# Output projection of a hybrid decoder layer by Strassen's seven products, weight sums formed on GpSimd beforehand

## The chip, the cores and the metric

One core of a Trainium2 chip runs the kernel. The metric is the device time of one execution in microseconds (us). Engines are named as in the profile: PE is TensorE (matmuls; PEld its weight loads), DVE VectorE, ACT ScalarE, POOL GpSimd, SP SyncE, which here issues most transfers. Each engine works through its own list of instructions in order; semaphores make it wait for the others.

## The reference, cut to what matters

```
h = rmsnorm(x, norm_pre_g)                      # x: 512 x 2048, float32
qa, ka, va, za, qb, ckv, zb, iq, ik, iw = split(h @ w_in)
o_a = diff_attention(qa, ka, va, ...)           # 8 heads: (softmax1 - lam*softmax2) @ v, rmsnorm of each head
o_b = dsa_attention(qb, ckv, iq, ik, iw, ...)   # 8 heads: 128 keys of 512 for each query, picked by an indexer
y = concat(o_a * silu(za), o_b * silu(zb)) @ w_out     # (512 x 2048) @ (2048 x 2048)
out = x + rmsnorm(y, norm_post_g)
```

Every weight is used in full float32 accuracy: a product A @ B is made as Ah@Bh + Ah@Bl + Al@Bh, where Ah is A rounded to the fast matmul format and Al the rest.

## The kernel before, in words

Everything is kept transposed, 128 features by 512 positions in a tile. **Weights** come in *units* of 128 x 1024 numbers (512 KB). `units` lists them in order of use; `load_to` issues the load from SP's queue (L98) into one of two tiles wf, `split_to` rounds it on ACT into wh (L124) and subtracts on DVE into wl (L125), `use` hands out the next pair and keeps three units split ahead. A weight tile and an activation tile give three matmuls.

**Stages.** First ckv, the index queries and keys, the 16 gates (tiles go0 to go15, SiLU applied), then 16 rounds that find the 128 best keys on DVE (L377, L378); before them POOL masks the three score tiles sc1 to sc3 (L371). Then 8 heads of group A (`head_a`): projections, two softmaxes, values into the PSUM bank av, and the norm of the head: PE sums squares (L518), DVE scales them (L193), POOL raises to the power -1/2 (`rstd`, L194, tile ro), PE spreads the four columns over the bank (`spread`, L200), and DVE multiplies into go[h]. Then 8 heads of group B (`head_b`). POOL has hardly anything else: the relative-bias strips go through DRAM tables that POOL writes early (L336).

**Output projection.** go0 to go15 are split into pairs hh, hl. Four column blocks n of 512; in each, 8 units of two 128-row weight tiles meet four position tiles i: 24 matmuls of 128x512 per unit (L606 to L608), 768 in all (some cut in halves of 256 columns at the very end). ACT squares a finished bank for the norm (L612), DVE multiplies it with the gain (L614). The last block goes position tile by position tile (L648 to L650), so that the norm, the scaled sum with x (L665) and the store (L666) of one tile run beside the matmuls of the next.

**Order of the work.** The program is written as straight code; a scheduler with tile dependencies and priorities places each instruction in its engine's list, so an engine that is free early gets later code early. In the loops over heads the code is written in the order projection, attention, norm.

Of the kernel before, what the change touches and what calls it, by code (L numbers as in the profile page):

```python
# [8 lines left out]
OP = mybir.AluOpType  # L9
# [16 lines left out]
def hybrid_layer(tc, xT, xn, wck, wT, wik, wva, wuv, wo, gpre, gpost, sub, kvg, ikg, lq1, lk1, lq2, lk2, relb, oneh, out):  # L26
    nc = tc.nc
    from contextlib import ExitStack
    with ExitStack() as st:
# [50 lines left out]
        for n in range(4):  # L80
            for kp in range(8):
                unit(wo[n, kp], (2, 512))
        stage, ready, flags = {}, {}, {"begin": None}
# [5 lines left out]

        def load_to(n):  # L90
            while pos["load"] < min(n, len(units)):
                i = pos["load"]
                ap, shp = units[i]
                c = shp[0] * shp[1]
                nm, bf = ("wf", 2) if flags["begin"] is not None else ("qk", 4)
                t = S.tile([128, 1024], F32, name=nm, bufs=bf)
                with tc.high_priority(lead()):
                    nc.sync.dma_start(t[:, :c], ap)  # L98
                stage[i] = t
                pos["load"] += 1  # L100

        last = [("qk", 4)] * 4 + [("v", 3)] * 3 + [("ck0", 1), ("ck1", 1)] + [("wh", 3), ("wl", 3)] * 3 + [("pt0a", 1)]

        def split_to(n):
            while pos["split"] < min(n, len(units)):
                i = pos["split"]
                load_to(i + 1)
                c = units[i][1][0] * units[i][1][1]
                t = stage.pop(i)
                names = [("wh", 3), ("wl", 3)]  # L110
                if i >= len(units) - 8:
                    names = [last.pop(0), last.pop(0)]
                w = []
                for nm, bf in names:
                    if nm == "pt0a":
                        w.append([S.tile([128, 512], F32R, name=x, bufs=1) for x in ("pt0a", "pt0b")])
                    else:
                        a = S.tile([128, 1024], F32R, name=nm, bufs=bf)
                        w.append([a[:, :512], a[:, 512:]] if units[i][1][1] == 512 else [a[:, :c]])
                m = c // len(w[0])  # L120
                with tc.high_priority(lead()):
                    for q in range(len(w[0])):
                        src = t[:, q * m:(q + 1) * m]
                        nc.scalar.copy(w[0][q], src)  # L124
                        nc.vector.tensor_tensor(w[1][q], src, w[0][q].bitcast(F32), op=OP.subtract)  # L125
                ready[i] = w
                pos["split"] += 1

        def use(ahead=3):
            i = pos["use"]  # L130
            pos["use"] += 1
            if ahead:
                load_to(i + ahead + 1)
                split_to(i + ahead)
            nk, n = units[i][1]
            w = ready.pop(i)
            per = nk // len(w[0])
            return [[w[a][k // per][:, (k % per) * n:(k % per + 1) * n] for k in range(nk)] for a in range(2)]
# [370 lines left out]
        def head_a(h, q, k, kl):  # L509
# [3 lines left out]
            sq = tmp("sq", 1)  # L513
# [38 lines left out]

        for h in range(8):
            next(sel, None)
            if h % 2 == 0:
                project_va(h // 2)
            t = scaled(proj_T(), 0.125)
            q = pair("qk", 4)
# [9 lines left out]
            next(sel, None)  # L568
            head_a(h, q, k, kl)
        for _ in sel:  # L570
            pass

        oh_, ol_ = [], []

        def split_o(m):
            a = S.tile([128, 512], F32R, name=f"hh{m}")
            b = S.tile([128, 512], F32R, name=f"hl{m}")
            split((a, b), go[m])
            oh_.append(a)
            ol_.append(b)  # L580

        for h in range(8):
            if h % 2 == 0:
                project_vb(h // 2)
            q = [project_qk(1.0 / 16), project_qk(1.0 / 16)]
            if h == 7:
                for m in range(15):
                    split_o(m)
            head_b(h, q)
        split_o(15)  # L590


        ssy = S.tile([128, 4, 4], F32, name="ssy")
        ys = {}
        for n in range(4):
            gB = S.tile([128, 512], F32, name="strip", bufs=2)
            nc.gpsimd.dma_start(gB, bcast(gpost[n], 512))
            if n % 2 == 0:
                banks = [proj_bank(), proj_bank(), proj_bank(), lg_bank()]
            else:  # L600
                banks = [lg_bank(), tr_bank(), tr_bank(), av_bank()]
            def part(kp, i, wh, wl):
                ts = slice(i * 128, (i + 1) * 128)
                for k in range(2):
                    kk = 2 * kp + k
                    nc.tensor.matmul(banks[i], oh_[kk][:, ts], wh[k], start=(kk == 0), stop=False)  # L606
                    nc.tensor.matmul(banks[i], oh_[kk][:, ts], wl[k], start=False, stop=False)  # L607
                    nc.tensor.matmul(banks[i], ol_[kk][:, ts], wh[k], start=False, stop=(kk == 15))  # L608

            def done(i):  # L610
                junk = S.tile([128, 512], F32, name="a3")
                nc.scalar.activation(junk, banks[i], AF.Square, accum_out=ssy[:, i, n:n + 1])  # L612
                y = S.tile([128, 512], F32, name=f"go{i * 4 + n}")
                nc.vector.tensor_tensor(y, banks[i], gB, op=OP.mult)  # L614
                ys[i, n] = y

            if n < 3:
                for kp in range(8):
# [3 lines left out]
                for i in range(4):  # L622
                    done(i)
                continue
            ws = []
            for i in range(4):
                xs = []
                for q in range(4):
                    xr = S.tile([128, 512], F32, name="e" if q < 2 else "tq", bufs=2)
                    nc.sync.dma_start(xr, xn[i * 128:(i + 1) * 128, q * 512:(q + 1) * 512])  # L630
                    xs.append(xr)
                y = S.tile([128, 512], F32, name=f"go{i * 4 + n}")
                ys[i, n] = y
                base = S.tile([128, 1], F32, name="base", bufs=2)
                nc.vector.tensor_reduce(base, ssy[:, i, :3], axis=mybir.AxisListType.X, op=OP.add)
                nc.vector.tensor_scalar(base, base, 1.0 / D, EPS, op0=OP.mult, op1=OP.add)
                ry = S.tile([128, 1], F32, name="ry", bufs=2)
                cuts = (0, 512) if i < 3 else (0, 256, 512)
                for a, b in zip(cuts, cuts[1:]):
                    o = (banks[i] if a == 0 else proj_bank())[:, a:b]  # L640
                    for kp in range(8):
                        if i == 0:
                            ws.append(use())
                        wh, wl = ws[kp]
                        for k in range(2):
                            kk = 2 * kp + k
                            ts = slice(i * 128, (i + 1) * 128)
                            nc.tensor.matmul(o, oh_[kk][:, ts], wh[k][:, a:b], start=(kk == 0), stop=False)  # L648
                            nc.tensor.matmul(o, oh_[kk][:, ts], wl[k][:, a:b], start=False, stop=False)
                            nc.tensor.matmul(o, ol_[kk][:, ts], wh[k][:, a:b], start=False,  # L650
                                             stop=(kk == 15))
                    junk = S.tile([128, 512], F32, name="a3")
                    sl = ssy[:, i, 3:4]
                    nc.scalar.activation(junk[:, :b - a], o, AF.Square, accum_out=sl)
                    nc.vector.scalar_tensor_tensor(ry if b == 512 else base, sl, 1.0 / D, base,
                                                   op0=OP.mult, op1=OP.add)
                    nc.vector.tensor_tensor(y[:, a:b], o, gB[:, a:b], op=OP.mult)
                nc.gpsimd.tensor_tensor(ry, ry, mhalf[:, 0:1], op=OP.pow)
                for q in range(4):
                    if i == 3 and q == 1:  # L660
                        t = S.tile([128, 512], F32, name="sq", bufs=1)
                        nc.scalar.activation(t, ys[i, q], AF.Copy, scale=ry)
                        nc.gpsimd.tensor_tensor(ys[i, q], t, xs[q], op=OP.add)
                    else:
                        nc.vector.scalar_tensor_tensor(ys[i, q], ys[i, q], ry, xs[q], op0=OP.mult, op1=OP.add)  # L665
                    nc.sync.dma_start(out[i * 128:(i + 1) * 128, q * 512:(q + 1) * 512], ys[i, q])  # L666
# [67 lines left out]
```

## Time and profile before

| | us |
|---|---|
| runs (3) | median 1059.06, 1058.71 to 1059.2 |
| profiled execution | 1059.01, its span 1057.1 |
| PE / DVE / ACT / POOL busy | 1043.6 / 567.5 / 421.2 / 35.0 |
| granted clock of PE, mean share of full speed | 0.996 |
| DMA | 116.09 MB, mean 110 GB/s |

Busy time of PE overlaps: a matmul of 512 columns is listed with 0.39 us, but the next one starts 0.23 us after it. "Chain" is the work that ended last, followed back from the end: a share of PE there is time that only PE could shorten. A name like pj or go is a tile; L is a line of the kernel before.

### The profile page before, as it was taken

How to read it: one execution, taken by the hardware profiler on the slowest of the kernel's cores; microseconds unless marked ns; L12 is line 12 of the kernel's file. 1: busy time of each engine (PE TensorE's matmuls, PEld its weight loads, DVE VectorE, ACT ScalarE, POOL GpSimd, SP SyncE). 2: the span in 40 equal slices, each digit the busy share in tenths (PEclk: the TensorE clock that was granted, in tenths of full speed). 3: DMA queues.
4: the chain of work that ended last, by engine and by line, in shares of the span. 5: the costliest groups of instructions: out<-in, count | busy, mean ns of one | idle time of the engine just before them, and what ended most of it. 6: DMA issues, size and time to landing. Idle time of an engine off the chain costs nothing.

```text
span 1057.1 us, 13923 instructions
## 1 busy us (share of the span) xinstructions
PE 1043.6 (99%) x5425; PEld 898.9 (85%) x5425; DVE 567.5 (54%) x1144; ACT 421.2 (40%) x789; POOL 35.0 (3%) x57
## 2 busy tenths in 40 slices
PE   8999999999999999999999999999999999999996
PEld 6798898888889899899899888888888888888886
DVE  5355554469953565465465466554645484323443
ACT  6543433332222564464365365332323353322320
POOL 2002100000000000000000000000000000000001
PEclk9999999999999999999999999999999999999999
DMA  8625723232333222222222232222222232333445
GB/s 295 237 97 152 250 100 100 100 100 80 100 100 100 85 85 91 80 90 80 91 90 70 90 99 91 71 97 73 90 80 90 80 100 90 101 100 110 139 130 189
DMA packets 37265, 116.09 MB, mean 110 GB/s; under 512 B 4592, under 2 KB 4720, under 8 KB 37200
## 3 DMA queue, kind: packets, MB, share of 16 engines
q1 hardware_dynamic: 35280, 108.68, 31.3%
q0 software_dynamic: 1920, 6.53, 2.2%
q8 instruction: 42, 0.69, 0.3%
q14 instruction: 23, 0.19, 0.1%
HBM read 110.96 MB, written 9.48 MB: 114 GB/s over the span
## 4 chain that ended last, share of the span: by engine, by line
PE 97%; DMA 1%; SPq 0%; DVE 0%; issue 0%; ACT 0%; DVEq 0%; POOL 0%; ACTq 0%; POOLq 0%
PE pj L161 19%; PE pj L160 19%; PE pj L159 19%; PE pj L451 3%; PE pj L450 3%; PE pj L449 3%; PE lg L534 3%; PE av L432 3%; PE pj L606 2%; PE pj L608 2%; PE pj L607 2%; PE lg L256 2%; PE lg L258 2%; PE tr L421 2%; PE lg L608 1%; PE lg L606 1%
## 5 line engine op out<-in xcount | busy, mean ns | idle before, releaser
L161 PE MATMUL pj<-hh,wl 128*128 128x512 f32 (+2 forms) x912 | 351.8, 386 | 0.0
L160 PE MATMUL pj<-hl,wh 128*128 128x512 f32 (+2 forms) x912 | 350.6, 384 | 0.0
L159 PE MATMUL pj<-hh,wh 128*128 128x512 f32 (+2 forms) x912 | 350.5, 384 | 0.0
L124 ACT CAST wh<-wf 128x1024 fp32r<-128x1024 f32 (+2 forms) x181 | 164.7, 923 | 394.9 <-PE pj L160 186.4
L125 DVE TENSOR_TENSOR wl<-wf,wh 128x1024 fp32r<-128x1024 f32 (+2 forms) x181 | 191.2, 1067 | 206.0 <-ACT wh L124 205.8
L161 PEld LDWEIGHTS pj<-hh,wl 128*128 128x128 f32 (+1 forms) x912 | 170.7, 187 | 30.8 <-issue 0.9
L160 PEld LDWEIGHTS pj<-hl,wh 128*128 128x128 f32 (+1 forms) x912 | 170.7, 187 | 30.1
L159 PEld LDWEIGHTS pj<-hh,wh 128*128 128x128 f32 (+1 forms) x912 | 170.8, 187 | 29.4
L451 PE MATMUL pj<-wh,hl 128*128 128x256 f32 x256 | 72.9, 285 | 0.0
L449 PE MATMUL pj<-wh,hh 128*128 128x256 f32 x256 | 72.9, 285 | 0.0
L450 PE MATMUL pj<-wl,hh 128*128 128x256 f32 x256 | 72.7, 284 | 0.0
L262 DVE SCALAR_TENSOR_TENSOR tq<-pj,rB 128x512 f32<-128x512 f32 (+1 forms) x40 | 26.5, 663 | 66.3 <-PE pj L161 64.6
L450 PEld LDWEIGHTS pj<-wl,hh 128*128 128x128 f32 x256 | 48.7, 190 | 0.6
L449 PEld LDWEIGHTS pj<-wh,hh 128*128 128x128 f32 x256 | 48.7, 190 | 0.4
L451 PEld LDWEIGHTS pj<-wh,hl 128*128 128x128 f32 x256 | 48.7, 190 | 0.1
L534 PE MATMUL lg<-ck,qk 128*128 128x256 f32 (+3 forms) x192 | 37.5, 322 | 0.0
L607 PE MATMUL pj<-wl,hh 128*128 128x512 f32 x96 | 37.5, 390 | 0.0
L606 PE MATMUL pj<-wh,hh 128*128 128x512 f32 x96 | 37.3, 391 | 0.0
L608 PE MATMUL pj<-wh,hl 128*128 128x512 f32 x96 | 37.2, 390 | 0.0
L534 PEld LDWEIGHTS lg<-ck,qk 128*128 128x128 f32 x192 | 32.0, 189 | 3.5
L544 ACT ACTIVATE a<-a,mx 128x128 f32<-128x128 f32 (+3 forms) x32 | 17.9, 560 | 38.6 <-DVE mx L543 38.6
L403 DVE SCALAR_TENSOR_TENSOR sc<-e,iw,sc 128x256 f32<-128x256 f32 (+2 forms) x45 | 27.7, 615 | 7.5 <-ACT e L399 4.9
(350 smaller groups left out, 1418.3 us busy)
## 6 DMA issues: line engine op xcount, KB each, us to landing
wf<-in_wT_dram SPq DMA_DIRECT2D x112, 512.0 KB, 3.5
wf<-in_wo_dram SPq DMA_DIRECT2D x32, 512.0 KB, 3.5
wf<-in_wva_dram SPq DMA_DIRECT2D x16, 512.0 KB, 3.5
table<-bd POOLq DMA_DIRECT2D x16, 320.0 KB, 9.9
go<-in_xT_dram SPq DMA_DIRECT2D x16, 256.0 KB, 6.9
v<-in_xn_dram SPq DMA_DIRECT2D x8, 512.0 KB, 5.9
strip<-table SPq DMA_DIRECT2D x16, 256.0 KB, 3.5
out_dram<-go SPq DMA_DIRECT2D x16, 256.0 KB, 3.7
```

The lines of the kernel that those rows point to most:

```text
L124: nc.scalar.copy(w[0][q], src)
L125: nc.vector.tensor_tensor(w[1][q], src, w[0][q].bitcast(F32), op=OP.subtract)
L159: nc.tensor.matmul(ps, a, x, start=(k == 0), stop=False)
L160: nc.tensor.matmul(ps, a, y, start=False, stop=False)
L161: nc.tensor.matmul(ps, b, x, start=False, stop=(k == KT - 1))
L449: nc.tensor.matmul(o, hh[kk][:, ts], wh[k], start=(kk == 0 and i % 2 == 0), stop=False)
L450: nc.tensor.matmul(o, hh[kk][:, ts], wl[k], start=False, stop=False)
L451: nc.tensor.matmul(o, hl[kk][:, ts], wh[k], start=False, stop=(kk == 15 and i % 2 == 1))
L534: nc.tensor.matmul(bank[:, :w], q[u][:, x, i * 128:(i + 1) * 128], ck[u][:, y, :w], start=(n == 0), stop=(n == 5))
L606: nc.tensor.matmul(banks[i], oh_[kk][:, ts], wh[k], start=(kk == 0), stop=False)
L607: nc.tensor.matmul(banks[i], oh_[kk][:, ts], wl[k], start=False, stop=False)
L608: nc.tensor.matmul(banks[i], ol_[kk][:, ts], wh[k], start=False, stop=(kk == 15))
```

## The change

y is 512 x 2048 and is now made in two column halves p of 1024. For each, A (positions by features) and B (features by columns) are cut in quarters, and seven products (Winograd's form) of 256 x 1024 by 1024 x 512 replace eight: P1 = A11 B11, P2 = A12 B21, P3 = S4 B22, P4 = A22 T4, P5 = S1 T1, P6 = S2 T2, P7 = S3 T3, with S1 = A21 + A22, S2 = S1 - A11, S3 = A11 - A21, S4 = A12 - S2.

The sums of weights (T1 to T4) don't depend on the input x. `combine(n)` makes them on POOL, 16 pieces of 128 x 512, each with four additions, five loads of 256 KB and four stores to DRAM tensors tw, all issued from POOL's queue and through two SBUF tiles wa and wb. Its steps stand in the code between the steps of the heads. The sums of activations: S1 is added after each head of group B; S2 to S4 are formed on POOL after the last head, two row pieces z and s3 at a time through pt0b and pt2a, then split. A unit now meets two position tiles, 12 matmuls; 56 units instead of 32, with a ring of seven buffers for the loads once the heads are done. DVE adds products from PSUM onto sums in SBUF, POOL adds two of the sums in SBUF.

```diff
+        def combine(n):
+            p, k = n // 8, n % 8
...
+            a, b = get(B22, "wa"), get(B12, "wb")
+            nc.gpsimd.tensor_tensor(b, a, b, op=OP.subtract)
+            put(3, b)
+            yield
+            a = get(B11, "wa")
+            nc.gpsimd.tensor_tensor(a, b, a, op=OP.add)
+            put(2, a)
+            yield
...
+        combos = (None for n in range(16) for _ in combine(n))
         for h in range(8):
             next(sel, None)
+            next(combos, None)
             if h % 2 == 0:
                 project_va(h // 2)
+                next(combos, None)
...
+        for j in range(8):
+            t = S.tile([128, 512], F32, name="pt0b")
+            s3 = S.tile([128, 256], F32, name="pt2a")
+            nc.gpsimd.tensor_tensor(t[:, up], go[j][:, up], go[j][:, lo], op=OP.subtract)
+            nc.gpsimd.tensor_tensor(t[:, lo], go[8 + j][:, lo], t[:, up], op=OP.subtract)
+            nc.gpsimd.tensor_tensor(s3, go[8 + j][:, up], t[:, up], op=OP.subtract)
+            z = S.tile([128, 2, 512], F32R, name=zhome[j][0], bufs=zhome[j][1])
+            split((z[:, 0, :], z[:, 1, :]), t)
...
+        def product(banks, form, u):
+            w = use()
+            for i in range(2):
+                part(banks[i], form, i, u, w)
...
-            if n < 3:
-                for kp in range(8):
-                    wh, wl = use()
-                    for i in range(4):
-                        part(kp, i, wh, wl)
+            P6, P3, P7 = two(), two(), two()
+            for u in range(4):
+                product(P6, "s2", u)
+                product(P3, "s4", u)
+                product(P7, "s3", u)
+            for i in range(2):
+                add(rc_[i], P6[i], ra[i])
+            for i in range(2):
+                add(rd[i], P3[i], rb_[i])
+                add(rd[i], rd[i], rc_[i], nc.gpsimd)
+                done(rd[i], i, n2, gBs[1])
...
+            for u in range(4):
+                product(P4, "a22", u)
+            for i in range(2):
+                base = head_of(2 + i, n1)
+                add(rc_[i], P4[i], rc_[i])
+                done(rc_[i], 2 + i, n1, gBs[0])
...
+                final(2 + i, ry, xs[2 + i])
+            w = [use() for u in range(4)]
+            for i in range(2):
...
+                    for u in range(4):
+                        part(bank, "a12", i, u, w[u], cs)
```

What it moves, first place: POOL's list around the power of the first heads of group A. Before, from the masks of the index scores on (sc is a score tile, ro the sums of squares of a head):

```order
L371 AFFINE_SELECT sc_587<-sc_587 128x128
L371 AFFINE_SELECT sc_588<-sc_588 128x128
L371 AFFINE_SELECT sc_589<-sc_589 128x128
L194 TENSOR_TENSOR ro<-ro,mhalf 128x4 x8
L597 DMA strip<-in_gpost_dram 128x512 x4
```

And now, around the power of the first head (L253 is the old L194; L146 loads a piece of w_out, L150 stores a sum):

```order
L146 DMA wb<-in_wo_dram 128x512
L165 TENSOR_TENSOR wb<-wb,wa 128x512
L253 TENSOR_TENSOR ro<-ro,mhalf 128x4
L150 DMA tw_93<-wb 128x512
L146 DMA wa<-in_wo_dram 128x512
L146 DMA wb<-in_wo_dram 128x512
L153 TENSOR_TENSOR wb<-wa,wb 128x512
L150 DMA tw_89<-wb 128x512
L146 DMA wa<-in_wo_dram 128x512
L157 TENSOR_TENSOR wa<-wb,wa 128x512
```

Of the 64 additions 28 now stand before the third mask, 52 before this power, 58 before the second head's and 63 before the third's.

Second place: DVE's list at the very end. Before, after the last half tile of the matmuls (L657 multiplies with the gain, L665 is the scaled sum with x):

```order
L657 TENSOR_TENSOR go_8947<-pj,strip 128x256
L665 SCALAR_TENSOR_TENSOR go_8106<-go_8106,ry,e 128x512
L665 SCALAR_TENSOR_TENSOR go_8662<-go_8662,ry,tq 128x512
L665 SCALAR_TENSOR_TENSOR go_8947<-go_8947,ry,tq 128x512
L730 UNCONDITIONAL_BRANCH
```

And now, from the sum with the last half tile of P2 (L731 adds a product, L762 is the old L665):

```order
L731 TENSOR_TENSOR hh_8884<-lg,hh_8884 128x256
L731 TENSOR_TENSOR base<-base,ssy 128x1
L748 TENSOR_SCALAR base<-base 128x1
L846 TENSOR_TENSOR hh_8884<-hh_8884,strip 128x256
L748 TENSOR_SCALAR base<-base 128x1
L752 SCALAR_TENSOR_TENSOR ry<-ssy,base 128x1
L752 SCALAR_TENSOR_TENSOR base<-ssy,base 128x1
L762 SCALAR_TENSOR_TENSOR go_8243<-go_8243,ry,hl_9354 128x512
L762 SCALAR_TENSOR_TENSOR go_8249<-go_8249,ry,hl_9355 128x512
L762 SCALAR_TENSOR_TENSOR hh_8883<-hh_8883,ry,hl_9356 128x512
L762 SCALAR_TENSOR_TENSOR hh_8889<-hh_8889,ry,hl_9357 128x512
L752 SCALAR_TENSOR_TENSOR ry<-ssy,base 128x1
```

Three scaled sums of the last position tile still follow; the four shown here belong to the tile before it, and now stand behind the last product's sum.

## Rows read from the trace of the kernel before

**Rows 1.** The page: busy us (share) xinstructions; shares of the chain.
```profile
PE 1043.6 (99%) x5425; PEld 898.9 (85%) x5425; DVE 567.5 (54%) x1144; ACT 421.2 (40%) x789; POOL 35.0 (3%) x57
...
PE 97%; DMA 1%; SPq 0%; DVE 0%; issue 0%; ACT 0%; DVEq 0%; POOL 0%; ACTq 0%; POOLq 0%
```
**Rows 2.** The chain in order of time, output projection: start us, us, what.
```profile
901.28 0.23 PE pj L606
...
911.94 0.23 PE lg L608
```
**Rows 3.** POOL in order of time: start us, us, engine, line [idle before <-releaser].
```profile
93.92 0.50 POOL L328 DMA_DIRECT2D bd<-v  x1 [7.51 <-DVE v L326]
96.10 4.17 POOL L336 DMA_DIRECT2D table<-bd  x8 [1.68 <-DMA bd<-v]
...
243.30 0.29 POOL L371 TENSOR_SCALAR_AFFINE_SELECT sc<-sc 128x128 f32<-128x128 f32 x1 [6.89 <-DVE sc L403]
401.96 1.47 POOL L194 TENSOR_TENSOR ro<-ro,mhalf 128x4 f32<-128x4 f32 x1 [158.37 <-DVE ro L193]
422.40 1.00 POOL L194 TENSOR_TENSOR ro<-ro,mhalf 128x4 f32<-128x4 f32 x1 [18.98 <-DVE ro L193]
482.53 1.45 POOL L194 TENSOR_TENSOR ro<-ro,mhalf 128x4 f32<-128x4 f32 x1 [59.12 <-DVE ro L193]
...
1051.36 1.74 POOL L663 TENSOR_TENSOR go<-sq,e 128x512 f32<-128x512 f32 x1 [0.83 <-ACT sq L662]
```
**Rows 4.** Line L200 (spread): duration ns min/median/max, first and last start us.
```profile
L200 PE MATMUL av<-ident,ro x32: 270/272/275, 405.2 to 678.8; 128*128 128x128 f32 x32
```
**Rows 5.** Line L597, four 256 KB loads from POOL's queue: landing after issue.
```profile
DMA to landing us min/median/max: 3.4/3.7/3.9
```
**Rows 6.** The page, DMA issues: xcount, KB each, median us to landing.
```profile
wf<-in_wo_dram SPq DMA_DIRECT2D x32, 512.0 KB, 3.5
...
table<-bd POOLq DMA_DIRECT2D x16, 320.0 KB, 9.9
...
pt0b<-in_oneh_dram POOLq DMA_DIRECT2D x1, 64.0 KB, 2.2
bd<-v POOLq DMA_DIRECT2D x1, 40.0 KB, 1.9
```
**Rows 7.** Line L666, sixteen 256 KB stores from SP's queue: landing after issue.
```profile
DMA to landing us min/median/max: 2.1/3.7/6.2
```
**Rows 8.** DVE in order of time, the end.
```profile
1050.57 0.75 DVE L665 SCALAR_TENSOR_TENSOR go<-go,ry,e 128x512 f32<-128x512 f32 x1 [0.39 <-POOL ry L658]
1051.24 2.41 DVE L665 SCALAR_TENSOR_TENSOR go<-go,ry,tq 128x512 f32<-128x512 f32 x2
```
**Rows 9.** DVE in order of time, at the first head's power.
```profile
401.79 0.74 DVE L505 SCALAR_TENSOR_TENSOR a<-a,sm,e 128x512 f32<-128x512 f32 x1
```
**Rows 10.** Stretches: us, busy PE, PEld, DVE, ACT, POOL, granted clock, DMA share, GB/s.
```profile
9.00:35.00 26.00, 24.73 (x101) 19.14 (x101) 15.43 (x27) 17.73 (x27) 0.00 (x0) 0.94 0.97 333
...
1049.00:1057.10 8.10, 0.14 (x2) 0.00 (x0) 3.58 (x5) 1.20 (x3) 2.28 (x2) 0.75 0.34 129
```
**Rows 11.** Groups by line and shape, DVE: xcount, busy us, mean ns, idle before.
```profile
L125 DVE TENSOR_TENSOR wl<-wf,wh 128x1024 fp32r<-128x1024 f32 x128 | 156.7, 1224 | 147.1 <-ACT wh L124 146.9
L125 DVE TENSOR_TENSOR wl<-wf,wh 128x512 fp32r<-128x512 f32 x52 | 33.7, 686 | 58.9 <-ACT wh L124 58.8
L238 DVE TENSOR_TENSOR hl<-go,hh 128x512 fp32r<-128x512 f32 x16 | 10.2, 680 | 0.7 <-ACT hh L237 0.7
...
L238 DVE TENSOR_TENSOR pt2b<-tr,pt2a 128x256 fp32r<-128x256 f32 x16 | 6.7, 420 | 0.6 <-ACT pt2a L237 0.6
```
**Rows 12.** PE in order of time, the last matmul.
```profile
1048.87 0.28 PE L650 MATMUL pj<-wl,hl 128*128 128x256 f32 x1
```
**Rows 13.** DVE in order of time, two scaled sums behind each other.
```profile
1028.35 1.41 DVE L665 SCALAR_TENSOR_TENSOR go<-go,ry,e 128x512 f32<-128x512 f32 x2
```

More of the change, by code (lines that the diff above doesn't have):

```diff
@@ L88, in lead @@
             return 0 if b is None else max(0, min(LEAD, tc.cur_priority - b))
+        ring = [("wf",), ("wf",)]
         def load_to(n):
-            while pos["load"] < min(n, len(units)):
+            while pos["load"] < min(n, len(units), flags["limit"]):
                 i = pos["load"]
@@ L512, in head_a @@
             values(pt, vh.pop(h), po)
-            sq = tmp("sq", 1)
+            sq = tmp()
             nc.scalar.activation(sq, po, AF.Square)
@@ L568, in hybrid_layer, with split_x @@
             next(sel, None)
+            next(combos, None)
             head_a(h, q, k, kl)
+            next(combos, None)
         for _ in sel:
             pass
[L573 to L580, printed above, removed]
+        lo, up = slice(0, 256), slice(256, 512)
+        xs_, F = [], {}
+        def split_x(j, cs):
+            if j == len(xs_):
+                xs_.append([S.tile([128, 512], F32R, name=f"{nm}{j}") for nm in ("hh", "hl")])
+            a, b = xs_[j]
+            split((a[:, cs], b[:, cs]), go[j][:, cs])
         for h in range(8):
@@ new lines, in hybrid_layer @@
+            if h == 6:
+                for _ in combos:
+                    pass
+            head_b(h, q)
+            next(combos, None)
+            eng = nc.gpsimd if h < 7 else nc.vector
+            eng.tensor_tensor(go[h][:, up], go[h][:, up], go[8 + h][:, up], op=OP.add)
+        flags["limit"] = len(units)
+        ring += [("ck1",)] + [(f"hh{j}", f"hh{j + 1}") for j in range(8, 16, 2)]
+        split_x(7, up)
+        zhome = [("qk", 4)] * 4 + [("v", 3)] * 3 + [("ck0", 1)]
+        whome = [("kz", 1), ("wa", 1), ("tq", 2), ("tq", 2), ("rB", 1), ("sc3", 1), ("pt0a", 1)]
@@ new lines, in hybrid_layer @@
+        ws_ = []
+        for nm, bf in whome:
+            if nm == "kz":
+                t = S.tile([128, 2, 2, 256], F32R, name=nm)
+                ws_ += [t[:, 0], t[:, 1]]
+            else:
+                ws_.append(S.tile([128, 2, 256], F32R, name=nm, bufs=bf))
+        for j in range(8):
[6 more added lines that the diff above has]
+            split((z[:, 0, :], z[:, 1, :]), t)
+            w = ws_[j]
+            split((w[:, 0, :], w[:, 1, :]), s3)
+            F["s4", j], F["s2", j] = ([z[:, x, cs] for x in range(2)] for cs in (lo, up))
+            F["s3", j] = [w[:, x, :] for x in range(2)]
@@ new lines, in hybrid_layer, with two @@
+        for j in range(8):
+            y = S.tile([128, 512], F32R, name=f"hl{8 + j}")
+            small = S.tile([128, 512], F32R, name=f"go{7 + j}" if j else "a3")
+            split((y, small), go[8 + j])
+            F["a12", j], F["a22", j] = ([y[:, cs], small[:, cs]] for cs in (lo, up))
+            F["a11", j], F["s1", j] = ([t[:, cs] for t in xs_[j]] for cs in (lo, up))
+        ring8 = [proj_bank, proj_bank, proj_bank, lg_bank, lg_bank, tr_bank, tr_bank, av_bank]
+        def two():
+            r = [ring8[0](), ring8[1]()]
+            ring8.extend(ring8[:2])
+            del ring8[:2]
+            return r
@@ new lines, in part @@
+        def part(bank, form, i, u, w, cs=slice(0, 512)):
+            wh, wl = w
+            ts = slice(i * 128, (i + 1) * 128)
+            for k in range(2):
+                kk = 2 * u + k
+                a, b = F[form, kk]
+                nc.tensor.matmul(bank, a[:, ts], wh[k][:, cs], start=(kk == 0), stop=False)
+                nc.tensor.matmul(bank, a[:, ts], wl[k][:, cs], start=False, stop=False)
+                nc.tensor.matmul(bank, b[:, ts], wh[k][:, cs], start=False, stop=(kk == 7))
@@ new lines, in more, with final @@
+        def more(dst, i, n, base):
+            nc.vector.scalar_tensor_tensor(dst, ssy[:, i, n:n + 1], 1.0 / D, base, op0=OP.mult, op1=OP.add)
+        def final(i, ry, xs):
+            nc.gpsimd.tensor_tensor(ry, ry, mhalf[:, 0:1], op=OP.pow)
+            for q in range(4):
+                if i == 1 and q == 1:
+                    t = S.tile([128, 512], F32, name="pt0b", bufs=1)
+                    nc.scalar.activation(t, ys[i, q], AF.Copy, scale=ry)
+                    nc.gpsimd.tensor_tensor(ys[i, q], t, xs[q], op=OP.add)
+                else:
+                    nc.vector.scalar_tensor_tensor(ys[i, q], ys[i, q], ry, xs[q], op0=OP.mult, op1=OP.add)
+                nc.sync.dma_start(out[i * 128:(i + 1) * 128, q * 512:(q + 1) * 512], ys[i, q])
```

244 lines of the change are left out of this document (149 added, 95 removed).

## The prediction, made before the changed kernel was run

> **What bounds the kernel now.** I read the page's busy times first, then the chain of waits, then the chain in order of time, then single engines in order of time. TensorE is busy 99% of the span and holds 97% of the chain that ended last [rows 1], so nothing but TensorE's own work can be taken out for a gain, and anything that makes TensorE wait is paid in full. In the output projection the chain is one matmul of 512 columns after another: 47 steps between 901.28 and 911.94 us, 0.227 us each [rows 2]. The listed 0.39 us of a matmul is longer because neighbours overlap; the step is the price. GpSimd does almost nothing, but what it does stands in TensorE's way: the power that makes each attention head's 1/rms (401.96 us for the first head), after which TensorE spreads that value over a bank at 405.2 [rows 3, 4]. TensorE takes its instructions in order, so it waits there for GpSimd.
>
> **What goes.** The projection has 720 matmuls of 512 columns and 96 of 256 in the order before, 648 and 48 in the new one. Counting two halves as one whole that is 768 against 672: 96 x 0.227 = 21.8 us less on the path. The stage is still 672 x 0.227 = 153 us, so the terms below decide how much of the saving is left.
>
> **What comes during the heads, and why it is not free.** 64 GpSimd additions of 128x512, each with one or two loads and one store of 256 KB on GpSimd's own queue. All use two tiles, wa and wb, so they form a chain in which a load waits for the last store of its tile. The scheduler has moved the chain to the front: the first rsqrt of a head now stands behind 52 additions, the second behind 58, the third behind 63. GpSimd works in order too. So the question is whether 63 additions are done when TensorE comes to the third head's spreading.
>
> Price of four additions (one column piece), each step from a row:
> - A load from GpSimd's queue lands 3.4 to 3.9 us after its issue, median 3.7 [rows 5]. I take 3.7; two of the five loads of a piece run right behind a store of the same queue, and eight tables issued back to back took 6.5 us and more [rows 6], so this is not the high end.
> - A 256 KB store from that queue is not in the trace. Nearest rows: 40 KB from the same queue 1.9 us [rows 6], 256 KB from SyncE's queue 2.1 to 6.2 us, median 3.7 with others queued [rows 7]. I take 2.9, between the lone 2.1 and the queued 3.7.
> - From a landing to GpSimd's next instruction 0.3 us: bd issued at 93.92 lands 1.9 later, at 95.8, and the first table goes out at 96.10 [rows 3, 6].
> - An addition of 128x512: one row, 1.74 us [rows 3]. It began at 1051.36 while VectorE was in an instruction with two SBUF inputs, and VectorE's pair of such instructions from 1051.24 took 2.41 us where one alone takes 0.75 [rows 8]. So they took turns: some 0.6 us of the 1.74 was waiting and 1.1 is the work; 2.41 = 0.7 + 1.1 + 0.6 fits. The first rsqrt shows the same: 1.47 us beside VectorE's 0.74 us instruction with two SBUF inputs that had begun 0.17 earlier, against 1.00 in the next head [rows 3, 9]. I take 1.35, VectorE being busy over half of the time; bounds 1.1 and 1.74.
> - An issue 0.53 (eight tables in 4.17) [rows 3].
>
> In a piece two loads wait for a store of the same tile, and four loads and four additions follow each other: 2 x (2.9 + 0.3) + 4 x 3.7 + 4 x (0.3 + 1.35 + 0.1) + 2 x 0.53 = 29.3 us, 7.3 per addition. Low: store 2.1, load 3.1 (below the lone 3.4, since the 40 and 64 KB rows land in 1.9 and 2.2), addition 1.1: 24.3, 6.1 each. High: 3.7, 3.9, 1.74: 33.2, 8.3 each.
>
> Where the chain must be: the third mask on the index scores has input at 243.30 [rows 3], and 28 additions stand before it, so at 7.3 us each and with the sixteen tables between, GpSimd is about there in time; I start from 246. Then the rest of one addition, 5, and 34 more: 246 + 5 + 34 x 7.3 = 499, and three powers, 502. TensorE was at the first spreading at 405.2 [rows 4]; the third power ran at 482.53, so the third spreading came near 485 [rows 3]. By a count of the matmuls ahead with their steps the new order comes 8 and 9 us earlier to these two, so at 397 and 476. GpSimd is late by 246 + 5 + 23 x 7.3 + 1.5 - 399 = 21 us at the first and 502 - 478 = 24 to 25 at the third (2 us of a later start allowed). The waits do not add up, since each shifts everything behind it: **+25 us**; bounds 0 (at 6.1: 458 + 3, in time) and 60 (at 8.3). Queued behind the waiting transposes on TensorE are the next head's projections, and VectorE and ScalarE wait for their banks in turn.
>
> The Trainium skill, DMA: Bandwidth & Descriptors (Anatomy of one DMA), gives a fit for one such DMA, about 2.0 us plus the bytes over 436 GB/s, which is 2.6 us for 256 KB, by estimate. The measured 3.4 to 3.9 us differ from it. By that rule the chain would be in time and this term nothing.
>
> **The other terms.**
> - Start: the first four loads and three stores fall into the first 50 us, and from 9 to 35 us the DMA engines are already 97% busy [rows 10]. 0.5 MB of loads ahead of the last x and weight tiles is 1.5 us at 333 GB/s: +2; bounds 0 and 5.
> - TensorE's granted clock was 0.94 in 9:35, after idle time, and 0.75 over the last 8 us, once the matmuls had ended [rows 10]. A wait of 20 us should cost the same fall: 26 x 0.06 = 1.6 us: +1.5; bounds 0 and 5 (three waits).
> - Sums of the activations: S2 to S4 are made piece by piece after the last head, GpSimd 3 x 8 additions of 256 columns through one tile pt0b, each piece then split by ScalarE and VectorE. TensorE needs them over 144 matmuls, 33 us. VectorE has, in the new order between the first and the last of them, 15 + 9 subtractions of 512 and 256 columns and 10 weight tiles, six whole at 1.22 and four in halves of 0.69: 15 x 0.68 + 9 x 0.42 + 10 x 1.3 + 1 = 28 us [rows 11]. GpSimd's 24 x 0.55 = 13 us exclude VectorE's instructions with two SBUF inputs, as seen above: 41 against 33 us. Part of it falls into VectorE's waits: +5; bounds 1 and 9.
> - End: before, the last result was scaled 4.7 us after the last matmul (1048.87 + 0.12; 2.41 us from 1051.24) [rows 8, 12]. Now two row tiles become ready at once after P4, 11 us before the end of TensorE, and VectorE has 2 + 3 full adds and scalings, 11 scaled sums of 0.70 [rows 13] and four half tiles behind each other; followed in order, the last scaled sum ends 8.1 us after the last matmul: +3.5; bounds 2 and 5.
> - Weight loads: 56 of 512 KB instead of 32, one per 2.7 us; a ring of seven buffers and landings of 3.5 us [rows 6] hide them; nothing.
>
> The Trainium skill, SBUF — State Buffer (Practical consequences), states the turns as a rule: a VectorE instruction with two SBUF inputs and a GpSimd instruction that reads SBUF exclude each other for the whole instruction. Rows 8 and 9 agree. It speaks against this change, which puts 64 + 24 such GpSimd instructions beside VectorE; without it the sums of the activations would cost 1 instead of 5.
>
> **Sum.** -21.8 + 25 + 2 + 1.5 + 5 + 3.5 = +15.2 us. The profiled execution took 1059.01 us (span 1057.1), 0.05 from the median of the runs, so 1074.
>
> **Rivals.**
> 1. The chain keeps up (6.1 us per addition: lone stores of 2.1, loads that land sooner without the 0.5 us steps between). For it: small transfers of that queue land in 1.9 to 2.2 us; 7.3 is only 10% over what the third head allows, (476 - 251) / 34 = 6.6. Against it: all four 256 KB loads of that queue took 3.4 or more. Time: 1059 - 21.8 + 2 + 5 + 3.5 = 1048, down to 1041 with the low ends.
> 2. The chain keeps up, but GpSimd and VectorE bind the projection at its start: 41 us where TensorE needs 33, and ScalarE's splits in the same loop through one pt0b. Price 9 to 14; decides from the point at which VectorE never idles there. 1059 - 21.8 + 2 + 12 + 3.5 = 1055.
> 3. Wait and saving cancel: about 10 us late at the third head, 6.8 us per addition: 1059.
> 4. The chain is much later, 8 us per addition and GpSimd late at the masks too: 1095 and over. This is the far end of my forecast.
>
> **Chances.** Forecast with rival 4: 0.60. Rival 1: 0.27, rival 2: 0.08, rival 3: 0.05. What a measurement of this kernel tells from no change is about 0.2%, 2 us. Faster: 0.35, same 0.05, slower 0.60. The forecast's own range is 1062 to 1098, from 7 to 8 us per addition; with rivals 1 and 2 the range is 1041 to 1098.
>
> **What would show it.** Right: TensorE idle before the spreading of the first to third head (transposes into av), released by GpSimd's power, 15 to 35 us in all, and none later; GpSimd's additions every 7 to 8 us from 246 us on. Shorter waits around the first sums, released by ScalarE or VectorE; VectorE scaling for some 8 us after the last matmul. Wrong: loads and stores of GpSimd that land in under 3 us, and a GpSimd that waits for VectorE before the first power; then the time is near 1048.

## The result, and the profile after

The changed kernel takes 1098.35 us (median of 4 runs, 1091.05 to 1103.19), the kernel before 1058.88 on the same chip: a ratio of 1.0357, 95% interval 1.033 to 1.0385. The forecast was 1074, with a range up to 1098. The sign was right, the size 24 us too small.

The page of the changed kernel; columns as in [rows 1]:

```profile
PE 1041.5 (95%) x5305; PEld 887.8 (81%) x5305; DVE 648.8 (59%) x1208; ACT 457.1 (42%) x835; POOL 247.8 (23%) x304
...
PE 54%; DMA 24%; POOL 10%; issue 7%; DVE 4%; ACT 1%; DVEq 0%; POOLq 0%; ACTq 0%
...
wb<-in_wo_dram POOLq DMA_DIRECT2D x48, 256.0 KB, 3.3
tw<-wb POOLq DMA_DIRECT2D x48, 256.0 KB, 2.4
wa<-in_wo_dram POOLq DMA_DIRECT2D x32, 256.0 KB, 3.5
```

TensorE held 97% of the chain before; now the loads, stores and additions of GpSimd's chain of sums hold about a third. GpSimd in order of time up to the first head's power (the place of [rows 3]):

```profile
380.81 1.29 POOL L157 TENSOR_TENSOR wa<-wb,wa 128x512 f32<-128x512 f32 x1 [2.66 <-DMA wa<-in_wo_dram]
...
404.32 1.29 POOL L153 TENSOR_TENSOR wb<-wa,wb 128x512 f32<-128x512 f32 x1 [2.57 <-DMA wb<-in_wo_dram]
405.91 0.55 POOL L150 DMA_DIRECT2D tw<-wb  x1 [0.30 <-POOL wb L153]
...
411.49 1.25 POOL L157 TENSOR_TENSOR wa<-wb,wa 128x512 f32<-128x512 f32 x1 [4.49 <-DMA wa<-in_wo_dram]
...
416.74 1.26 POOL L161 TENSOR_TENSOR wb<-wb,wa 128x512 f32<-128x512 f32 x1 [2.61 <-DMA wb<-in_wo_dram]
...
423.84 1.26 POOL L165 TENSOR_TENSOR wb<-wb,wa 128x512 f32<-128x512 f32 x1 [2.39 <-DMA wb<-in_wo_dram]
425.06 1.03 POOL L253 TENSOR_TENSOR ro<-ro,mhalf 128x4 f32<-128x4 f32 x1
```

The power stands behind the additions, and TensorE behind the power. TensorE's waits over the whole span: line, releaser, us in total, times, longest:

```profile
PE av L259 <- POOL ro L253: 20.0, 1, 20.0
PE lg L315 <- ACT e L458: 3.7, 2, 3.3
PE tr L577 <- ACT tq L573: 3.4, 5, 0.7
PE lg L719 <- DVE wl L186: 2.9, 4, 1.0
PE lg L218 <- ACT hh L235: 2.8, 1, 2.8
```

Only the first row was in the forecast. The second belongs to the masks: GpSimd came to them 12 us later than before (three masks from 241.33 to 255.41 us; the last was at 243.30 [rows 3]), and VectorE, which takes in what TensorE makes there, stood still until the first:

```profile
241.67 0.43 DVE L436 MAX8 m<-sc 128x8 f32<-128x256 f32 x1 [9.39 <-POOL sc L430]
```

The third row (the squares of a first head's values, tile tq) I had not seen at all. The clock around the long wait, columns as in [rows 10]:

```profile
405.90:426.20 20.30, 0.32 (x4) 0.17 (x3) 1.00 (x3) 0.49 (x2) 8.16 (x11) 0.60 0.32 103
426.20:432.00 5.80, 5.80 (x33) 5.80 (x34) 2.29 (x5) 1.44 (x3) 1.57 (x3) 0.64 0.28 93
```

The last matmul starts at 1080.68 us instead of 1048.87 [rows 12], and from there to the end of the span it is 17.4 us instead of 8.2. Where the 32 us ahead of the last matmul are, I read from the matmuls themselves: for each, the time from its start to the next one's, less the usual step for its width (0.227 us for 512 columns), summed by stretch, after less before. Start (to 30 us) +3.4; 30 to 230 us -0.9; masks (230 to 260) +3.6; 260 to 400 +1.8; first spread and the clock behind it (400 to 440) +23.4; 440 to 716 +12.7; 716 to 930 +0.3; sums of the activations (930 to 990) +9.1; then +0.5. That is +53.9, and with -21.8 for the products +32.1, where the last matmul's start says 31.8.

### The profile page after: what moved, and what is told of

Read it like the earlier page. It is cut to its first block, busy times and chain, and to the rows that moved or that the text cites. A ratio compares the mean times of both kernels' runs of the same rounds, so it can differ in the third digit from the quotient of the medians.

```text
span 1098.1 us, 14286 instructions
## 1 busy us (share of the span) xinstructions
PE 1041.5 (95%) x5305; PEld 887.8 (81%) x5305; DVE 648.8 (59%) x1208; ACT 457.1 (42%) x835; POOL 247.8 (23%) x304
## 4 chain that ended last, share of the span: by engine, by line
PE 54%; DMA 24%; POOL 10%; issue 7%; DVE 4%; ACT 1%; DVEq 0%; POOLq 0%; ACTq 0%
DMA wb<-in_wo_dram 12%; PE pj L218 9%; PE pj L219 9%; PE pj L220 9%; DMA tw<-wb 6%; DMA wa<-in_wo_dram 4%; PE lg L593 3%; PE av L491 2%; PE pj L508 2%; PE pj L509 2%; PE pj L510 2%; POOL wb L161 2%; POOL wb L165 2%; POOL wb L153 2%; POOL wa L157 2%
## 5 line engine op out<-in xcount | busy, mean ns | idle before, releaser
L186 DVE TENSOR_TENSOR wl<-wf,wh 128x1024 fp32r<-128x1024 f32 (+1 forms) x150 | 187.5, 1251 | 152.1 <-ACT wh L185 151.8
L185 ACT CAST wh<-wf 128x1024 fp32r<-128x1024 f32 (+1 forms) x150 | 154.9, 1033 | 285.9 <-PE pj L219 96.7
L186 DVE TENSOR_TENSOR wl<-hh,wh 128x512 fp32r<-128x512 f32 x56 | 45.9, 863 | 15.0 <-ACT wh L185 14.9
L253 POOL TENSOR_TENSOR ro<-ro,mhalf 128x4 f32<-128x4 f32 x8 | 8.4, 1053 | 195.7 <-DVE ro L252 195.7
L509 PEld LDWEIGHTS pj<-wl,hh 128*128 128x128 f32 x256 | 51.2, 200 | 0.5
L670 POOL TENSOR_TENSOR go<-go,go 128x256 f32<-128x256 f32 x7 | 6.4, 917 | 169.7 <-DVE go L610 168.7
L185 ACT CAST wh<-hh 128x512 fp32r<-128x512 f32 x56 | 31.6, 618 | 25.0 <-PE lg L720 7.5
L146 POOL DMA_DIRECT2D wb<-in_wo_dram x48 | 26.2, 546 | 66.8 <-DMA tw<-wb 65.6
L593 PE MATMUL lg<-ck,qk 128*128 128x384 f32 (+3 forms) x192 | 37.6, 322 | 0.0
L462 DVE SCALAR_TENSOR_TENSOR sc<-e,iw,sc 128x256 f32<-128x256 f32 (+2 forms) x45 | 32.7, 728 | 5.8 <-ACT e L458 3.5
```

The costliest lines, as they stand in the source:

```text
L146: nc.gpsimd.dma_start(t, wo[p, x, k // 2][:, cs])
L185: nc.scalar.copy(x, t)
L186: nc.vector.tensor_tensor(y, t, x.bitcast(F32), op=OP.subtract)
L462: nc.vector.scalar_tensor_tensor(sc[i], re[:, :w], iw[:, i - 1, h:h + 1], sc[i], op0=OP.mult, op1=OP.add)
L509: nc.tensor.matmul(o, hh[kk][:, ts], wl[k], start=False, stop=False)
L593: nc.tensor.matmul(bank[:, :w], q[u][:, x, i * 128:(i + 1) * 128], ck[u][:, y, :w], start=(n == 0), stop=(n == 5))
```

## The experiments

Theories of what costs most: 1, the place of GpSimd's chain; 2, its bytes and its turns with VectorE, wherever it stands; 3, the projection's own sums and end. 4 (the squares' buffer), 5 (VectorE's backlog at the end) and 6 (the sums of the activations) came with what the runs showed. "Gaps at the sums" are the steps beyond the usual, 880 to 960 us, as above. "End" is from the last matmul's start to the end of the span, in the profiled execution. Ratios are to the kernel before, run beside each; not all rows come from the same chip, so rows are compared by their ratios. By the intervals a difference between two rows is known to some 2 to 5 us.

| run | median us | ratio (95%) | last matmul | end | gaps at the sums |
|---|---|---|---|---|---|
| changed kernel | 1098.35 | 1.0357 (1.033 to 1.0385) | 1080.7 | 17.4 | 9.1 (930 to 990) |
| e1_paced | 1070.54 | 1.0096 (1.0072 to 1.0121) | 1046.7 | 17.6 | 9.3 |
| e2_no_sums | 1067.91 | 1.0076 (1.0061 to 1.0091) | 1050.4 | 15.4 | 9.3 |
| e3_sums_in_before | 1096.65 | 1.0362 (1.0339 to 1.0384) | 1083.1 | 10.4 | none |
| e4_tail | 1102.38 | 1.0393 (1.0352 to 1.0433) | 1079.5 | 19.8 | 9.2 (930 to 990) |
| e5_sq_in_before | 1076.71 | 1.0155 (1.0125 to 1.0185) | 1062.6 | 8.2 | none |
| e6_paced_sq | 1057.45 | 0.9975 (0.9963 to 0.9987) | 1036.1 | 17.6 | 9.1 |
| e7_paced_seq | 1067.71 | 1.0078 (1.0052 to 1.0105) | 1056.0 | 14.5 | 9.5 (to 975) |
| e8_paced_early | 1073.77 | 1.0135 (1.011 to 1.0159) | 1058.2 | 17.4 | 11.0 (to 990) |
| e9_end | 1054.73 | 0.9959 (0.9946 to 0.9973) | 1038.0 | 16.6 | 9.2 |
| e10_s_dve | 1054.62 | 0.9959 (0.9946 to 0.9971) | 1035.8 | 17.5 | 7.8 |
| e11_all | 1052.23 | 0.9931 (0.9918 to 0.9945) | 1034.2 | 13.9 | 7.8 |
| e12_no_low | 1052.26 | 0.9934 (0.9911 to 0.9956) | 1032.9 | 17.6 | 4.4 |
| e13_no_s | 1057.47 | 0.9958 (0.9926 to 0.999) | 1030.3 | 17.5 | 0.9 |
| e14_sq | 1084.66 | 1.0232 (1.019 to 1.0274) | 1062.1 | 17.5 | 9.5 (to 975) |

**e1_paced.** Each piece's first load waits for a small copy into its tile that reads the last power:

```
+            a = S.tile([128, 512], F32, name="wa")
+            if flags.get("hold") is not None:
+                nc.gpsimd.tensor_copy(a[:, :4], flags.pop("hold"))
...
             rstd(ro, ss, 128)
+            flags["hold"] = ro
...
             head_a(h, q, k, kl)
-            next(combos, None)
+            piece(4 + h)
```

> The changed kernel with its 64 additions held to the heads: four pieces (of four additions) start behind the first masks at about 240 us, one piece starts behind the power of each of the first eight heads, four more follow in the first four of the second heads; the work is the same. Theory 1 (what costs is where GpSimd's in-order chain stands: ahead of the masks and the first powers, from 10 us on): the 20 us wait of TensorE at the first spread and the 3.7 us gap at 240 go, the start is 3 us shorter, and some of the 13 us lost between 440 and 716 us goes with them; 1054 to 1067. Theory 2 (what costs is what the chain moves and reads, its bytes and its turns with VectorE, wherever it stands): 1085 or more. Theory 3 (most of the loss is in the output projection's sums and end): 1085 or more, and the gaps between 930 and 990 and the 17 us end unchanged.

1070.5, 28 us less with the same work, 3.5 above theory 1's range. The first power now waits for nothing but its input, and TensorE never waits for it:

```profile
392.63 1.04 POOL L257 TENSOR_TENSOR ro<-ro,mhalf 128x4 f32<-128x4 f32 x1 [34.85 <-DVE ro L256]
```

Theories 2 and 3 fall as the main cause. The five waits for the squares stay, and so do the gaps at the sums and the end.

**e2_no_sums.** `t = lambda x, u: unit(wo[p, x - 1, u], ...)` and no `combine`.

> The changed kernel without the weights' combinations: no load, addition or store on GpSimd, and the four combined forms are read as plain quarters of the same size (so the products use other weights). The rest is as it was. Theories 1 and 2 (all that is lost before the projection, some 44 us by the steps of the matmuls, hangs on the chain): 1050 to 1057. Theory 3 (the projection's own sums and its end lose most): 1085 or more. Between the two, about 1065, if the 13 us between 440 and 716 us come from another order of the matmuls that stays.

1067.9, the third case: 440 to 716 us lose 11.4 us here too, without any sum (12.7 in the changed kernel). Against e1_paced, the sums in a good place cost 2.6 us by the medians; the intervals overlap, so it can be nothing.

**e3_sums_in_before.** `combine` and its calls in the kernel before, and the squares in tq as in the change.

> The kernel before with the chain alone: the same 64 loads, additions and stores on GpSimd at the same places of the program, stored and never used; the output projection is as before (768 matmuls). Theories 1 and 2: 1095 to 1105, with a wait for the power of about 20 us ahead of the first spread. Theory 3: 1070 or less.

1096.7, and a wait for the power:

```profile
PE av L233 <- POOL ro L227: 16.0, 1, 16.0
```

It has the chain and the shared buffer, the two that are taken apart below, and none of the new products.

**e4_tail.** `if i > 1 or q == 1 and i == 1:` ahead of the ScalarE scaling and GpSimd addition.

> The changed kernel with the last scaling and residual sum of the row blocks 2 and 3 (8 VectorE instructions of 0.7 us) done as a ScalarE scaling and a GpSimd addition instead. Theory (VectorE's queue sets the end: eight final instructions stand ahead of the last bank's addition, which begins 3 us after the last matmul): the end behind the last matmul falls from 17.4 to 12 to 14 us, the time by 3 to 6. Rival (the end hangs on GpSimd additions of 1.3 to 2.2 us that now follow one another, 8 of them, and on turns with VectorE): the end stays at 16 to 20 us, no gain. The stretch ahead of 1040 us is as in the changed kernel in both.

The rival: the end grew to 19.8 us.

**e5_sq_in_before.** One line in the kernel before:

```
-            sq = tmp("sq", 1)
+            sq = tmp()
```

> The kernel before with one edit of the change alone: the squares of a first head's values go into a buffer of the ring tq (two buffers, shared with the scaled projections) and no more into one of their own. Theory 4 (this edit, which I had not priced, is what loses 13 us between 440 and 720 us, also where no sum of weights is made: the next scaled projection has to wait for the squares, so fewer projections can be put between the transposes): 1066 to 1073, with five or more gaps of about 1 us ahead of L577's successor. Rival (the order of the matmuls there comes from another part of the change): 1058 to 1061, no gaps.

1076.7; +1.55%, more than I had expected. TensorE's waits from 380 to 720 us: the kernel before has none that the view lists; this kernel has

```profile
PE tr L518 <- ACT tq L514: 3.4, 5, 0.7
PE tr L421 <- DVE a L505: 1.2, 1, 1.2
PE av L432 <- ACT pt0a L237: 0.6, 1, 0.6
```

which are the changed kernel's, line for line. TensorE in order of time there:

```profile
627.25 0.28 PE L471 MATMUL pj<-wh,ck 128*128 128x256 f32 x1
628.73 0.44 PE L421 MATMUL tr<-ident,a 128*128 128x128 f32 x2 [1.19 <-DVE a L505]
629.73 0.49 PE L432 MATMUL av<-pt0a,v 128*128 128x512 f32 x1 [0.56 <-ACT pt0a L237]
...
632.49 0.28 PE L432 MATMUL av<-pt3a,v 128*128 128x128 f32 x1
633.45 0.72 PE L518 MATMUL tr<-onec,tq 128*128 128x1 f32 x5 [0.69 <-ACT tq L514]
```

The transposes and the products with the values stand there bare, with no matmuls of a projection between them. The ring tq has two buffers, and in program order the squares and two scaled projections of the next head take turns in it. So the second of these has to wait for the squares' release, and the projections that used to fill TensorE's waits are ordered elsewhere. By the steps this costs 3.1 us from 260 to 400 and 11.4 from 440 to 716. The listed waits from 380 to 720 are 6.1 of it. Behind groups of them TensorE also runs at its lower clock for a while, 0.50 of full speed or 1.2 GHz, though it is busy throughout; the kernel before has none of that there:

```profile
392.70:396.10 3.40, 3.40 (x18) 3.40 (x17) 2.62 (x4) 2.46 (x4) 1.03 (x1) 0.51 0.00 0
635.10:638.50 3.40, 3.40 (x13) 3.01 (x13) 2.28 (x5) 1.76 (x3) 1.01 (x1) 0.50 0.00 0
679.50:682.90 3.40, 3.40 (x9) 2.64 (x8) 2.69 (x6) 1.22 (x2) 1.01 (x1) 0.50 0.00 0
```

The heads' spreads come earlier for it: the first at 397.6 us, where the kernel before has 405.2 [rows 4].

**e6_paced_sq.** e1_paced and `sq = S.tile([128, 512], F32, name="a3")`.

> The kernel of the paced additions (1070.5) with the squares in the buffer a3, which is dead by then, instead of tq. Theory 4: the gaps of 0.7 to 1.5 us in the first heads go, 1056 to 1062. Rival: 1068 to 1072.

As theory 4 says: no wait from 380 to 720 us, 13 us less, and 0.25% below the kernel before. The first spread is back at 404.9.

**e7_paced_seq.** For the second column half, `for b, f in ((P6, "s2"), (P3, "s4"), (P7, "s3")): for u in range(4)`.

> The paced kernel with the three middle products of the second column half one after the other (P6, P3, P7, with their weights in that order) instead of interleaved by weight tile; the same matmuls. Theory 5 (the end is VectorE's backlog: three products end together at 24 us before TensorE's end, and 12 sums and scalings, eight weight splits and eight final instructions come at once; now six of them come 11 to 22 us earlier): the end behind the last matmul falls from 17.6 to 9 to 12 us, 1061 to 1065. Rival (the last row's own chain of instructions sets it): 16 us or more, 1068 to 1072.

Between the two: the end falls by 3.1 us to 14.5, not to 9 to 12. The intervals of the times overlap e1_paced's.

**e8_paced_early.** P4 and P2 ahead of P6, P3, P7 in the first half.

> The paced kernel with P4 and P2 of the first column half ahead of P6, P3 and P7, so that TensorE has 44 us of products that need no activation sum, not 22, while GpSimd makes S2 to S4; P4 waits in two spare tiles, two more copies on ScalarE. Theory 6 (the 9 us of gaps at the projection's start are S2 to S4 and their splits not keeping up with 33 us of products): the gaps between 880 and 960 us fall from 9 to 1 to 4, 1062 to 1066. Rival (VectorE's instructions there are too many in any order, with its weight splits): 6 or more of the 9 us stay, at P4 and P2, 1067 to 1072.

The rival: the gaps stay, now at P4 and P2 (11.0 us). That the time is worse is not shown, since the intervals overlap.

**e9_end.** `if i == 3 or i == 1 and q == 1:`, and one power `ry2` for row blocks 0 and 1.

> The kernel with the paced additions and the squares in a3 (1057.5), with the end in another order: the scaled sums of row block 3 on ScalarE and GpSimd, and those of row block 0 behind those of row block 1's last sum (one power for both blocks). The same matmuls. Theory 5 (VectorE works in order, and eight scaled sums of other row blocks, 5.4 us, stand ahead of the last bank's addition and of the last row block's square sum): the end behind the last matmul falls from 17.6 to 10 to 13 us, 1050 to 1053. Rival (the backlog is there anyway, and what is moved comes back as GpSimd's turns, as when two row blocks were moved): 16 us or more, 1056 or more.

The end is 16.6: the rival was right on it, though the median lies below its bound; the intervals of e6_paced_sq and e9_end overlap. VectorE in order of time, then GpSimd's additions at the same time:

```profile
1040.71 0.26 DVE L750 TENSOR_SCALAR base<-base 128x1 f32<-128x1 f32 x2
1040.89 1.12 DVE L754 SCALAR_TENSOR_TENSOR ry<-ssy,base 128x1 f32<-128x1 f32 x1
...
1042.26 1.21 DVE L754 SCALAR_TENSOR_TENSOR base<-ssy,base 128x1 f32<-128x1 f32 x1
```

```profile
1040.73 1.26 POOL L766 TENSOR_TENSOR hh<-e,sc 128x512 f32<-128x512 f32 x1
1041.95 1.51 POOL L766 TENSOR_TENSOR hh<-e,pt0a 128x512 f32<-128x512 f32 x1
```

An instruction of one column ends with GpSimd's addition: 1.21 us instead of the 0.16 that the same one takes in the changed kernel (below). Four such instructions between 1038 and 1044 us take 4.1 us instead of 0.6, so some 3.5 of the 5.4 us taken off VectorE came back.

**e10_s_dve.** S2 to S4 with `nc.vector` instead of `nc.gpsimd`.

> The same base (1057.5), with S2 to S4 made by VectorE instead of GpSimd (24 instructions of 256 columns, 0.42 us each instead of GpSimd's 0.73 to 1.05). Theory 6a (turns: GpSimd's 20 us there shut VectorE out for as long, so VectorE, busy over 92%, is relieved by 10 us although it gets 10 us of work): the gaps between 880 and 960 us fall from 9 to 3 to 6, 1051 to 1055. Rival 6b (VectorE has simply too many instructions there, and more make it worse): 9 us or more, 1057 to 1064.

The gaps went to 7.8, between the theories; the time is in theory 6a's range, but its interval overlaps that of e6_paced_sq.

**e11_all.** e6_paced_sq with the edits of e7, e9 and e10.

> All of it together on the changed kernel: paced additions, squares in a3, S2 to S4 on VectorE, the end in another order and the middle products of the second column half one after the other. If the terms add up (28 + 13 for the heads, 3 to 6 for the sums, 5 to 9 for the end, the saving of 21.8 kept): 1043 to 1050, 1% below the kernel before. Rival (6b, and the end hangs on VectorE's backlog whatever the order): 1056 to 1062.

1052.2: 0.7% below the kernel before, 4.1% below the change by the ratios, the best of those that make the whole output. It lies between the two ranges: the terms add up less well than hoped.

**e12_no_low.** `split((y, small), ...)` becomes `nc.scalar.copy(y, go[8 + j])`.

> The base of 1057.5 (paced additions, squares in a3) without the low parts of the last eight gated values (8 VectorE instructions of 512 columns, 5.5 us; the high parts are used twice): nothing else is left out. Theory 6b (VectorE has too much to do in the first 54 us of the projection, weight splits included, and each of its instructions counts): the gaps between 880 and 960 us, 9 us in the base, fall to 3 to 6, 1051 to 1055. Theory 6a (GpSimd's turns and its slow sums alone): 8 or more stay, 1056 to 1058.

**e13_no_s.** `t, s3 = go[8 + j], go[j][:, up]` in place of the three subtractions.

> The same base without the 24 GpSimd subtractions that make S2 to S4 (the splits read the gated values as they are). The 16 splits on ScalarE and VectorE stay. Theory 6a: the gaps fall from 9 to 1 to 3, 1049 to 1052, since VectorE gets back the 20 us in which GpSimd shuts it out. Theory 6b: 5 or more stay, 1053 to 1057.

Gaps 4.4 and 0.9: taking away 5.5 us of VectorE's own work removes half, taking away GpSimd's sums nearly all. The same 54 us of e6_paced_sq, then of e10_s_dve, then of e13_no_s, columns as in [rows 10]:

```profile
896.00:950.00 54.00, 50.20 (x205) 37.10 (x204) 51.42 (x60) 29.90 (x53) 30.14 (x26) 1.00 0.46 139
```

```profile
896.00:950.00 54.00, 50.48 (x208) 38.14 (x209) 50.27 (x83) 29.66 (x54) 6.72 (x5) 1.00 0.43 141
```

```profile
896.00:950.00 54.00, 54.00 (x239) 44.20 (x238) 40.29 (x55) 26.44 (x44) 6.86 (x5) 1.00 0.58 188
```

VectorE is 95% busy with GpSimd's 30 us beside it, 75% without. In e10_s_dve it makes the sums itself, 24 instructions of 0.42 us, some 10 us of work, and is busy for 1 us less than in e6_paced_sq: the turns with GpSimd had cost it about 11 us (an estimate from these rows). Both theories hold in part: VectorE is at its limit, and either the turns or the sums as its own work put it there. The ten runs of e13_no_s spread from 1048.3 to 1060.7 us and the profiled one took 1049.6, so its gaps are used here and not its median.

**e14_sq.** The changed kernel with the squares in a3.

> The changed kernel with the squares in a3 alone; the additions stand unpaced as in the change. With it the four cases of paced or not and squares shared or not are complete. If the two losses add up (28 and 13): 1083 to 1087, with the wait of TensorE at the first spread of 20 us still there. If the shared squares only cost where the additions don't hold TensorE anyway: 1090 to 1098. If without the shared buffer TensorE comes to the spreads earlier and waits longer: 1088 or more, and waits also at the second or third head.

They add up, within what the intervals can tell. Sharing the buffer costs 0.0125 of the time with the additions unpaced (1.0357 to 1.0232) and 0.0121 with them paced (1.0096 to 0.9975); their place costs 0.0261 and 0.0257. TensorE waits for two powers, the first head's and the third's:

```profile
PE av L259 <- POOL ro L253: 19.4, 2, 18.1
```

## Why the prediction was wrong

- Products, -21.8: right. e6_paced_sq comes near it: -21.8, sums 9, end 9.4 make -3.4; measured -0.25%, 2.6 us.
- **The chain late, +25, with start +2 and clock +1.5**: right in mechanism, and the size in part by luck. By e14_sq and e6_paced_sq its place costs 0.0257 x 1059 = 27 us, give or take 5; forecast 28.5. An addition every 7.2 us (380.81 to 423.84, six steps), 7.3 forecast. Stores land in 2.4 us and loads in 3.3 to 3.5, both shorter than I took, but 0.30 us pass between an addition's end and its store's issue, and GpSimd waits up to 4.49 us for one of the loads shown. The luck: the sum puts the first power at 419 us and TensorE at 399 ahead of its spread; they came at 425.06 and 406.1, both 6 to 7 us later, TensorE mostly for the masks and the start, and so the wait was 20.0 where 21 was forecast. It came at the first head alone: for the third head a wait of 24 to 25 in all was forecast, but once TensorE had waited, GpSimd was in time there. The Trainium skill, DMA: Bandwidth & Descriptors (Anatomy of one DMA), gave 2.6 us for such a DMA by estimate; the stores (2.4) come near it, the loads (3.3 and 3.5) don't.
- The masks, for which GpSimd was put at "about there in time", cost 3.6 us: it was 12 us late. e1_paced loses nothing there, so they are part of the 27.
- **The squares' buffer, not priced at all: 13 us.** This is the step that failed. The sum has no term for it, and the Strassen products have no part in it: one line of the diff moves `sq` into tq, and that line alone costs the kernel before 1.55%, 16 us (e5_sq_in_before); undone, it gives back 13 (e6_paced_sq, e14_sq). I followed the two tiles that the additions bring and missed the one that is taken away. The new order of TensorE's instructions has the transposes bare there, which could be read ahead. The sum even holds a sign of it: the 8 us by which I counted the first spread earlier are this buffer's doing, for that spread starts at 397.6 us with the shared buffer alone, and at 404.9 without it in e6_paced_sq. I took the earlier start as a fact of the order and did not ask which matmuls had gone from in front of it.
- Sums of the activations, +5 of 1 to 9: mis-sized, 9.1. The count of 41 us of VectorE and GpSimd against TensorE's 33 is 8 over, near what came, but I took part of it off for VectorE's waits, and they are short: in the 35.8 us from GpSimd's first sum to its last VectorE was busy for 33.7. One of its terms was wrong: no run shows the 0.55 us per sum; the 24 took 25.7 us, 1.07 each with their turns and 0.73 at the least, and not 13. Rival 2's mechanism was there, beside the late chain. The Trainium skill, SBUF — State Buffer (Practical consequences), states the turns as a rule; the trace agrees, since from 880 to 960 us a weight split of 128x512 takes 0.93 us in the mean in e6_paced_sq and 0.78 in e13_no_s, without the sums.
- End, +3.5 of 2 to 5: mis-sized, +9.2. VectorE at the end of the changed kernel, in order of time:

```profile
1083.43 0.75 DVE L762 SCALAR_TENSOR_TENSOR hh<-hh,ry,pt0a 128x512 f32<-128x512 f32 x1
1084.09 0.42 DVE L731 TENSOR_TENSOR hh<-lg,hh 128x256 f32<-128x256 f32 x1
...
1085.07 0.16 DVE L752 SCALAR_TENSOR_TENSOR base<-ssy,base 128x1 f32<-128x1 f32 x1
1085.83 1.42 DVE L762 SCALAR_TENSOR_TENSOR go<-go,ry,hl 128x512 f32<-128x512 f32 x2 [0.60 <-POOL ry L755]
1087.16 1.41 DVE L762 SCALAR_TENSOR_TENSOR hh<-hh,ry,hl 128x512 f32<-128x512 f32 x2
1088.49 0.15 DVE L752 SCALAR_TENSOR_TENSOR ry<-ssy,base 128x1 f32<-128x1 f32 x1
...
1090.09 2.42 DVE L762 SCALAR_TENSOR_TENSOR hh<-hh,ry,hl 128x512 f32<-128x512 f32 x2
```

  Scaled sums of other row blocks stand ahead of the last bank's addition (1084.09) and of the last block's 1/rms (1088.49). The last one ends 11.7 us after the last matmul, not 8.1, and the stores take 5.6 more, not 3.4 [rows 8, 10]. The three edits of e11_all brought the end to 13.9; what holds it there is not taken apart.

Sum as measured: -21.8 + 27 + 13 + 9 + 9 = +36; the median says +39.5, the profiled execution +41. The rest is within what the ratios can tell. Of the 24 us between forecast and result the squares' buffer is 13, the end 6 and the sums 4.

## What to carry to other kernels

Price the buffers that a diff takes away as carefully as the work that it adds: one tile moved to a shared ring cost more than half of what the matmuls saved. Work put on an idle engine is nearly free only behind that engine's urgent instructions; give it a dependency that holds it there, where the scheduler would put the chain ahead of them, as it did here with 52 of 64 additions. Where instructions of two engines shut each other out, count their times as one sum for the stage.

## What the runs showed of the hardware

- A GpSimd addition of 128x512 holds off even a one-column VectorE instruction with two SBUF inputs until it ends (1.21 us instead of 0.16, e9_end).
- The granted clock falls after short gaps too. In the changed kernel, four waits that add up to 2.7 us idle in 7.2:

```profile
657.00:664.20 7.20, 4.53 (x29) 3.44 (x27) 4.78 (x9) 3.75 (x9) 0.00 (x0) 1.00 0.21 77
664.20:671.00 6.80, 6.80 (x33) 6.01 (x34) 5.63 (x9) 4.94 (x9) 1.01 (x1) 0.75 0.07 12
```

  are followed by a mean of 0.75 with TensorE busy throughout: half of that stretch is at the lower of the two levels, 1.2 GHz. In e6_paced_sq, without such gaps, the granted clock stays at 1.00 from 380 to 720 us.
- Among the runs of one kernel the mean granted clock differs, and the time with it: from 0.982 to 0.976 over the changed kernel's four (1091.05 to 1103.19 us), from 0.994 to 0.987 over the ten of e13_no_s (1048.3 to 1060.7). The runs of the kernel before spread over 1 to 4 us. What makes the clock differ is open.
